# Linear attention in one kernel of two transformer blocks: both heads of a level written into two PSUM banks, their products alternating between the row halves of the tensor engine, with new scheduling priorities

## Chip, cores and metric

One Trainium2 chip, one of its cores. The metric is the device time of one execution in microseconds (us), as the median of several runs.

## What is computed

The program runs two blocks one after the other on 256 tokens of width 1024, in float32, with two layers in each block. The first block mixes three attentions per layer and is touched by the change only through the order of its instructions. In the second block a layer projects its input, hands the pieces to three mixers (GLA, a gated linear attention; RWKV7, a delta-rule recurrence; NSA, a sparse attention), joins their outputs in one output projection, and ends with a feed-forward network. GLA is what the change rewrites:

```python
def _gla_mixer(q, k, v, g, a_lr, w_a2, b_a, ln_w, ln_b):
    log_a = jax.nn.log_sigmoid((a_lr @ w_a2 + b_a).astype(f32)) / GLA_TAU
    ...
    def step(state, inp):
        qi, ki, vi, ai = inp
        b = jnp.cumsum(ai, axis=2)
        inter = jnp.einsum('bhtk,bhkv->bhtv', qi * jnp.exp(b), state)
        diff = b[:, :, :, None, :] - b[:, :, None, :, :]
        decay = jnp.exp(jnp.where(causal, diff, -jnp.inf))
        scores = jnp.einsum('bhtk,bhsk,bhtsk->bhts', qi, ki, decay)
        intra = jnp.einsum('bhts,bhsv->bhtv', scores, vi)
        ...
    o = _head_norm(o, ln_w, ln_b, H, LN_EPS)
    return (o * jax.nn.silu(g.astype(f32))).astype(dt)
...
        mix = jnp.concatenate([o_gla, o_rwkv, o_nsa], axis=-1) @ w_out[l]
```

## The kernel before

Nearly all of the time is matrix products on the tensor engine (PE). A float32 product with a weight is split into three products of a high and a low part (`mm3`, L353 to L357), and ScalarE (ACT) and VectorE (DVE) split each weight tile (`whi` at L321, `wlo` at L298) before it is used. L298 is a helper for all two-operand vector operations and L446 one for all transposes, so both lines collect many operations, and the names of the tiles tell them apart.

A framework orders the instructions. Each instruction gets a priority from its place in the program and from a table of offsets, `AHEAD`: a section opened with `self.sec("x")` is moved ahead by the number under "x", and it is moved back when that is negative. In a layer of the second block (`block2_layer`) four generators, for RWKV7, GLA, NSA's direct part and NSA's compressed part, are stepped by `side_by_side`: the one with the smallest clock goes next, and a generator's `yield d` moves its own clock by d. What the scheduler makes of it is a fixed order of instructions on each engine. Whatever stands behind a waiting instruction on its engine waits too.

GLA handles its 256 tokens without a chunk loop. `gla` (L1217) goes through eight levels, m = 1, 2, 4, ..., 128; in level m a block of 2m tokens attends from its upper half to its lower half. A level makes the tile `g_E`: two subtractions on DVE, an exponential on ACT (L1245), two multiplications on DVE, by `g_q` and `g_k`. The four heads of 64 channels lie in two tiles of 128 partitions (index c) by two halves of 64 partitions (index j). A product contracts over 64 partitions, so it uses half the rows of PE: rows 0 to 63 for j = 0, rows 64 to 127 for j = 1. For each j, four products (two token tiles tt by two c; L1258, and L1256 in the level m = 64; two in the level m = 128) go into one PSUM bank, and the new entries are then merged into `g_S[j]`, which holds the scores: by a masked copy on DVE (L1266) in the first five levels, by copies on ACT in the last three (L1263, L1260, L1270). When all levels are done, twelve products (L1277, L1278) make GLA's output o, `head_norm` (L877 to L893, with one operation on POOL at L890) and a multiplication by `g_g` make `yg`, and `out_feat` (L1169) transposes `yg` and splits it for the output projection. RWKV7 does the same with `yr`, and NSA with `yn`.

PSUM has eight banks. In the second block two of them form a pair for the pool `pp`, two a pair for `pr`, three are single banks (`pa`) and one is `pg`, which `psg` hands out. `psp` hands out one bank of the pair `pp`, `two` both of them. The projections, the RWKV7 levels and the output projection use the pair too: the output projection accumulates its four output pieces in two banks of `pa` and in the two banks of the pair `pp`, and its inputs come in the order NSA's two halves, `yr`, `yg`. In the kernel before, GLA has the bank `pg` for its levels, for o and for the transposes of `yg`.

```python
            for j in range(2):
                pr = slice(64 * j, 64 * j + 64)
                ps = self.psg(2, 2, 128)
...
                yield 2
        o = self.psg(2, 256)
```

Of the kernel before, what the change touches and what calls it, by code (L numbers as in the profile page):

```python
# [151 lines left out]
class Kern:  # L152
# [1047 lines left out]
    def gla_decay(self, alr, P):  # L1200

        nc = self.nc
        z = self.low_rank(self.psg, P, P_TAIL, 64, 80, alr)
        zb = self.c3("g_z")
        for c in range(2):
            nc.vector.tensor_scalar(zb[:, c], z[:, c], P[:, P_BA + c:P_BA + c + 1], None, op0=ALU.add)
        az = self.c3("g_az")
        nc.scalar.activation(az, zb, AF.Abs)
        nc.scalar.activation(az, az, AF.Exp, scale=-1.0)
        nc.scalar.activation(az, az, AF.Ln, bias=1.0)  # L1210
        self.stt(zb, zb, 0.0, az, ALU.min, ALU.subtract)
        b = self.c3("g_b")
        for c in range(2):
            nc.vector.tensor_tensor_scan(b[:, c], self.one.to_broadcast([128, 256]), zb[:, c], 0.0, ALU.mult, ALU.add)
        return b

    def gla(self, ins, b, rows, out):  # L1217

        nc = self.nc
        mm = nc.tensor.matmul  # L1220
        cst = self.c
        q, k, v, g2 = ins
        ST = [self.u("g_S", 2, 2, 128) for j in range(2)]
        qk = self.c3("g_E")
        nc.gpsimd.tensor_tensor(out=qk, in0=q, in1=k, op=ALU.mult)
        ps = self.psg(2, 2, 2)
        for tt in range(2):
# [9 lines left out]
        for lv in range(8):  # L1237
            m = 1 << lv
# [8 lines left out]
            self.tt_(view(E, 0), view(E, 0), view(k, 0), ALU.mult)  # L1247
            for j in range(2):
                pr = slice(64 * j, 64 * j + 64)
                ps = self.psg(2, 2, 128)  # L1250
                self.busy(f"gla{j}", ps[:, 0], ps[:, 1])
                for tt in range(2 if m < 128 else 1):
                    for c in range(2):
                        a, e = (E[pr, c, 128 * t:128 * t + 128] for t in ((tt, tt) if m < 128 else (0, 1)))
                        if m == 64:
                            mm(ps[0:64, tt, c, 0:64], a[:, 0:64], e[:, 64:128], start=tt + c == 0, stop=tt + c == 2)  # L1256
                        else:
                            mm(ps[:, tt, c], a, e, start=tt + c == 0, stop=c == 1 and (tt == 1 or m == 128))  # L1258
                if m == 64:
# [9 lines left out]
                else:  # L1269
                    nc.scalar.copy(off[:, j], ps[:, 0])  # L1270
                yield 2
        o = self.psg(2, 256)
        for h in range(4):
            j, c = h % 2, h // 2
# [211 lines left out]
    def block2_layer(self, l, xT):  # L1486
        nc = self.nc
        P = self.act.tile([128, P_N], F32, name="P2")
# [37 lines left out]
        def gla():  # L1526
            yield from self.gla_inputs(l, xT.w, made["g"])
            b = self.gla_decay(tl, P)
            yield 6
            for t in self.gla(made["g"], b, rows, yg):  # L1530
                yield t
            with self.sec("ofg"):
                feats["g"] = self.out_feat([yg[:, 0], yg[:, 1]], 0.5, self.psg)

# [191 lines left out]
}.items() for n in names.split()}  # L1726
AHEAD = dict(x=-107, x2=-267, m01=254, n12=1422, h1=368, n3=-94, rwkv=0, cmp=0, w=-330, h2=785, ww=-366, out=-225, gla=0, ofg=442, ln2=18, atta=-78, tok=336, imask=-209, rx1=-82, attb=590, rxf=526, w1=15, feat=5, nsa=0, ofn=326, rx0=25, hw=499, ofr=-116, hd=675, rin=10, wo=-72, ln1=298, t_side=-3, t_group=8, t_gin=20, t_gla=0, t_dir=-5, t_cmp=-10, side=-42)
KEEP = dict(lev=2, nsa=1, gla0=0, gla1=0, wo=3, rms00=0, rms01=0, rms10=0, rms11=0, ln100=0, ln101=0, ln110=0, ln111=0, ln200=0, ln201=0, ln210=0, ln211=0, start=0)
# [72 lines left out]
```

## Time and profile before

| | before |
|---|---|
| three runs, us | 1562.68, 1556.77, 1562.52; median 1562.52 |
| the profiled execution, us | 1556.73; its span 1554.9; mean granted clock of PE 0.988 |
| PE busy | 1492.6 us, 96% of the span |
| weight loads of PE (PEld) | 1286.2 us, 83% |
| DVE busy | 938.9 us, 60% |
| ACT busy | 710.6 us, 46% |
| POOL busy | 50.0 us, 3% |
| DMA | 231.69 MB, 149 GB/s on average |

How to read it: busy times are sums over one execution, on engines that run at the same time, so they don't add up to the span. PE's busy time is near the span, but its ends are modelled and products are pipelined, so what a product costs is read from the distance between the starts of neighbours, not from its own duration. A float32 product appears as two records. The three runs lie at two levels, one near the profiled execution and one 5.8 us above it.

### The profile page before, as it was taken

The page shows a single profiled execution, that of the slowest core. Times are in us where ns is not written, and L with a number is a line of the kernel's source. Part 1 is how long each engine was busy: PE and PEld are TensorE (multiplying, and loading weights), DVE is VectorE, ACT ScalarE, POOL GpSimd, SP SyncE. Part 2 cuts the span into 40 slices and gives each one's busy share as a digit, 9 for nine tenths or more (in the row PEclk, how much of TensorE's full clock was granted, in tenths as well). Part 3 has the DMA queues.
Part 4 walks back from the last instruction along what each step waited for, and adds up shares of the span by engine and source line. Part 5 has one row for each costly group of instructions (what it writes and reads, how often), then busy time and mean ns, then how long its engine had stood idle before and what let it go on. Part 6 is the DMA issues. An engine that isn't in the chain of part 4 may idle for free.

```text
span 1554.9 us, 26032 instructions
## 1 busy us (share of the span) xinstructions
PE 1492.6 (96%) x10502; PEld 1286.2 (83%) x10502; DVE 938.9 (60%) x1531; ACT 710.6 (46%) x1286; POOL 50.0 (3%) x82
## 2 busy tenths in 40 slices
PE   6999999999999999999999989999999999899997
PEld 5877899988787999868767769998888677789986
DVE  5586565565686655565367475556754675755564
ACT  5545554445454444444454334444454544344451
POOL 0000000000000000000011010000000010100000
PEclk9999999999999999999999999999999999999999
DMA  7743435445444445556710245556447101445560
GB/s 254 235 147 122 150 122 189 158 156 180 166 149 131 149 136 182 167 152 201 249 34 2 80 142 176 188 172 224 139 146 254 42 1 42 144 164 191 181 215 27
DMA packets 72984, 231.69 MB, mean 149 GB/s; under 512 B 8736, under 2 KB 11552, under 8 KB 72864
## 3 DMA queue, kind: packets, MB, share of 16 engines
q1 hardware_dynamic: 67248, 219.74, 42.8%
q10 hardware_dynamic: 5616, 10.30, 2.1%
q8 instruction: 82, 1.34, 0.3%
q14 instruction: 38, 0.31, 0.1%
HBM read 228.96 MB, written 1.05 MB: 148 GB/s over the span
## 4 chain that ended last, share of the span: by engine, by line
PE 46%; DVE 4%; DMA 3%; ACT 2%; issue 1%; POOL 0%; DVEq 0%; ACTq 0%; SPq 0%
PE ps L357 10%; PE ps L355 10%; PE ps L356 10%; PE ps L353 4%; DMA raw<-in_stream_dram 2%; PE ps L446 2%; PE ps L1258 2%; PE ps L613 1%; PE ps L656 1%; DVE wlo L298 1%; ACT whi L321 1%; PE ps L438 1%; PE ps L867 1%; PE ps L1052 0%; PE ps L1001 0%
## 5 line engine op out<-in xcount | busy, mean ns | idle before, releaser
L298 DVE TENSOR_TENSOR wlo<-raw,whi 128x1024 fp32r<-128x1024 f32 (+2 forms) x364 | 428.1, 1183 | 313.3 <-ACT whi L321 306.2
L321 ACT CAST whi<-raw 128x1024 fp32r<-128x1024 f32 (+2 forms) x364 | 367.8, 1018 | 403.9 <-PE ps L356 206.4
L355 PE MATMUL ps<-xTh,whi 128*128 128x256 f32 x720 | 205.5, 285 | 4.4 <-ACT whi L321 4.4
L357 PE MATMUL ps<-xTh,wlo 128*128 128x256 f32 x720 | 205.5, 285 | 1.5 <-DVE wlo L298 1.5
L356 PE MATMUL ps<-xTl,whi 128*128 128x256 f32 x720 | 205.1, 285 | 0.0
L357 PE MATMUL ps<-hTh,wlo 128*128 128x256 f32 x640 | 182.4, 285 | 0.0
L355 PE MATMUL ps<-hTh,whi 128*128 128x256 f32 x640 | 181.7, 284 | 0.0
L356 PE MATMUL ps<-hTl,whi 128*128 128x256 f32 x640 | 181.5, 284 | 0.0
L355 PEld LDWEIGHTS ps<-xTh,whi 128*128 128x128 f32 x720 | 138.8, 193 | 6.1 <-ACT whi L321 4.8
L357 PEld LDWEIGHTS ps<-xTh,wlo 128*128 128x128 f32 x720 | 138.8, 193 | 2.0 <-DVE wlo L298 1.9
L356 PEld LDWEIGHTS ps<-xTl,whi 128*128 128x128 f32 x720 | 138.7, 193 | 0.8
L356 PEld LDWEIGHTS ps<-hTl,whi 128*128 128x128 f32 x640 | 122.6, 191 | 1.1 <-issue 0.7
L355 PEld LDWEIGHTS ps<-hTh,whi 128*128 128x128 f32 x640 | 122.6, 192 | 0.7
L357 PEld LDWEIGHTS ps<-hTh,wlo 128*128 128x128 f32 x640 | 122.6, 192 | 0.4 <-issue 0.3
L355 PE MATMUL ps<-whi,hTh 128*128 128x512 f32 (+2 forms) x256 | 97.3, 380 | 1.1 <-ACT wi L772 1.1
L357 PE MATMUL ps<-whi,hTl 128*128 128x512 f32 (+2 forms) x256 | 97.0, 379 | 0.0
L356 PE MATMUL ps<-wlo,hTh 128*128 128x512 f32 (+2 forms) x256 | 95.9, 375 | 0.8 <-DVE wlo L298 0.8
L355 PE MATMUL ps<-whi,xTh 128*128 128x512 f32 (+1 forms) x144 | 55.1, 383 | 4.0 <-ACT xTh L425 2.5
L355 PEld LDWEIGHTS ps<-whi,hTh 128*128 128x128 f32 x256 | 48.1, 188 | 11.8 <-issue 3.3
L355 PE MATMUL ps<-whi,f_h 128*128 128x512 f32 x144 | 57.1, 396 | 0.0
L356 PE MATMUL ps<-wlo,f_h 128*128 128x512 f32 x144 | 57.0, 396 | 0.0
L357 PE MATMUL ps<-whi,f_l 128*128 128x512 f32 x144 | 56.9, 395 | 0.0
(474 smaller groups left out, 2898.1 us busy)
## 6 DMA issues: line engine op xcount, KB each, us to landing
raw<-in_stream_dram SPq DMA_DIRECT2D x346, 512.0 KB, 4.2
raw<-in_stream_dram SPq DMA_DIRECT2D x56, 256.0 KB, 3.1
whi<-in_stream_dram SPq DMA_DIRECT2D x11, 512.0 KB, 5.9
wlo<-in_stream_dram SPq DMA_DIRECT2D x11, 512.0 KB, 6.5
row<-in_ln_w_dram ACTq DMA_DIRECT2D x8, 256.0 KB, 4.0
row<-in_ln_b_dram ACTq DMA_DIRECT2D x8, 256.0 KB, 4.6
raw<-in_stream_dram SPq DMA_DIRECT2D x4, 480.0 KB, 3.8
raw<-in_stream_dram SPq DMA_DIRECT2D x4, 420.0 KB, 5.4
```

The source lines that it names most:

```text
L298: self.nc.vector.tensor_tensor(out=out, in0=a, in1=b, op=op)
L321: nc.scalar.copy(hi[:, :b - a], raw)
L353: mm(out, a, b, start=start, stop=stop)
L355: mm(out, a[0], b[0], start=start, stop=False)
L356: mm(out, a[0], b[1], start=False, stop=False)
L357: mm(out, a[1], b[0], start=False, stop=stop)
L438: self.nc.tensor.matmul(o, self.negb, self.causb[:, None, :].to_broadcast([128, n, 128]), start=True, stop=True)
L446: self.nc.tensor.transpose(pt[:, j], s, self.ident)
L613: nc.tensor.matmul(o[:, ocol(h)], ps[:, i * nk + k, :], vt(k, h), start=first and i == 0 and k == 0, stop=last and i == nh - 1 and k == nk ...
L656: nc.tensor.matmul(s3[:, i], qT[pr, h // 2], kT(pr, h, 128 * nk), start=i == 0, stop=False)
L867: self.nc.tensor.matmul(ps[:, c], P[r0:r1, off + 128 * c:off + 128 * c + 128], rhs[r0:r1], start=c == 0, stop=c == 1)
L1258: mm(ps[:, tt, c], a, e, start=tt + c == 0, stop=c == 1 and (tt == 1 or m == 128))
```

## The change

1. The low-rank decay of GLA, the diagonal of the scores, o and the transposes of `yg` move from the bank `pg` to a bank of the pair `pp`.
2. In a level both heads j get a bank each, the two banks of the pair `pp`, and j becomes the innermost loop: the eight products of a level (four in the last) alternate between the rows 0 to 63 and the rows 64 to 127 of PE. The merging operations of both heads follow, and one `yield 4` takes the place of two `yield 2`. The removed `busy` calls issued nothing (their counts in `KEEP` are 0).
3. Eight numbers of `AHEAD` change, so that the order changes in the first block, at the start and in GLA.

```diff
-        z = self.low_rank(self.psg, P, P_TAIL, 64, 80, alr)
+        z = self.low_rank(self.psp, P, P_TAIL, 64, 80, alr)
...
-        ps = self.psg(2, 2, 2)
+        ps = self.psp(2, 2, 2)
...
-            for j in range(2):
-                pr = slice(64 * j, 64 * j + 64)
-                ps = self.psg(2, 2, 128)
-                self.busy(f"gla{j}", ps[:, 0], ps[:, 1])
-                for tt in range(2 if m < 128 else 1):
-                    for c in range(2):
+            two = [p.rearrange("p (a b k) -> p a b k", a=2, b=2) for p in self.two(self.pp)]
+            for tt in range(2 if m < 128 else 1):
+                for c in range(2):
+                    for j in range(2):
+                        pr = slice(64 * j, 64 * j + 64)
                         a, e = (E[pr, c, 128 * t:128 * t + 128] for t in ((tt, tt) if m < 128 else (0, 1)))
                         if m == 64:
-                            mm(ps[0:64, tt, c, 0:64], a[:, 0:64], e[:, 64:128], start=tt + c == 0, stop=tt + c == 2)
+                            mm(two[j][0:64, tt, c, 0:64], a[:, 0:64], e[:, 64:128], start=tt + c == 0, stop=tt + c == 2)
                         else:
-                            mm(ps[:, tt, c], a, e, start=tt + c == 0, stop=c == 1 and (tt == 1 or m == 128))
+                            mm(two[j][:, tt, c], a, e, start=tt + c == 0, stop=c == 1 and (tt == 1 or m == 128))
+            for j, ps in enumerate(two):
...
-                yield 2
-        o = self.psg(2, 256)
+            yield 4
+        o = self.psp(2, 256)
...
-                feats["g"] = self.out_feat([yg[:, 0], yg[:, 1]], 0.5, self.psg)
+                feats["g"] = self.out_feat([yg[:, 0], yg[:, 1]], 0.5, self.psp)
```

Of `AHEAD` these change: x2 -267 to 185, gla 0 to -9, atta -78 to -518, tok 336 to 241, feat 5 to 7, rx0 25 to 45, ofr -116 to -604, t_gin 20 to 28. In the changed kernel the products of the levels are at L1257 (m = 64: L1255); nearly all other lines keep their numbers.

What moves, at three places of the first layer of the second block. An order says what stands behind what on an engine, and in brackets which engines' semaphores an instruction waits for.

First place: PE, in the GLA levels. Before, from one head of a level over other work to the next head (L656 and L659 are NSA's scores, L446 `r_P` transposes of RWKV7, L1064 its products):

```order
L1258 MATMUL ps<-g_E 128x128 [waits DVE_49]
L1258 MATMUL ps<-g_E 128x128 x3
L656 MATMUL ps<-n_kw,n_qT 128x256 x2
L659 LDWEIGHTS negb
L659 MATMUL ps<-causb,negb 128x2x128
L446 MATMUL ps<-c_ident,r_P 128x128 [waits DVE_49]
L446 MATMUL ps<-c_ident,r_P 128x128 x3
L1258 MATMUL ps<-g_E 128x128 [waits DVE_49]
L1258 MATMUL ps<-g_E 128x128 x3
L1064 MATMUL ps<-r_P,r_M 64x64 [waits Activation_49]
```

Now, the second and the third level (L1102 and L1106 are products of RWKV7's solution, `pexp` belongs to NSA):

```order
L1257 MATMUL ps<-g_E 128x128 [waits DVE_49,PE_49,Activation_49]
L1257 MATMUL ps<-g_E 128x128 x7
L1102 MATMUL ps<-r_rhs,r_Q 64x64 [waits PE_49,Activation_49]
L1102 MATMUL ps<-r_rhs,r_Q 64x64 x7
L446 MATMUL ps<-c_ident,pexp 128x128 x2
L656 MATMUL ps<-n_kw,n_qT 128x256 x2
L1257 MATMUL ps<-g_E 128x128 [waits DVE_49,PE_49]
L1257 MATMUL ps<-g_E 128x128
L1106 MATMUL ps<-r_WU,r_M 64x64 [waits DVE_49]
L1106 MATMUL ps<-r_WU,r_M 64x64 x3
L1257 MATMUL ps<-g_E 128x128 x3
```

The four products of a head have become the eight of a level. The levels now begin after the last RWKV7 level (the last L1064); before, the first five of them lay between its levels. Two levels, the third and the sixth, are broken into pieces by other work.

Second place: DVE, the masked copies. Before, from the first head of the second level to the second head of the third:

```order
L1266 COPY_PREDICATED g_S<-c_mgla,ps 128x512 [waits PE_49,Pool_49]
L298 TENSOR_TENSOR g_E<-g_b 128x32x8 x2
L298 TENSOR_TENSOR r_P<-ps,r_P 128x2x4x64 [waits PE_49]
L298 TENSOR_TENSOR g_E<-g_E,g_q 128x32x8 [waits Activation_49]
L1266 COPY_PREDICATED g_S<-c_mgla,ps 128x512 [waits PE_49]
L298 TENSOR_TENSOR g_E<-g_E,g_k 128x32x8 [waits DVE_49]
L595 TENSOR_REDUCE mx<-ps 128x2 [waits PE_49]
L597 TENSOR_SCALAR nb<-mx 128x2 [waits DVE_49]
L1266 COPY_PREDICATED g_S<-c_mgla,ps 128x512 [waits PE_49]
```

Now, the first and the second level:

```order
L1266 COPY_PREDICATED g_S<-c_mgla,ps 128x512 [waits PE_49,Pool_49]
L1266 COPY_PREDICATED g_S<-c_mgla,ps 128x512 [waits Pool_49]
L298 TENSOR_TENSOR g_E<-g_E,g_q 128x64x4 [waits Activation_49]
L298 TENSOR_TENSOR g_E<-g_E,g_k 128x64x4 [waits DVE_49]
L298 TENSOR_TENSOR g_E<-g_b 128x32x8 x2
L298 TENSOR_TENSOR g_E<-g_E,g_q 128x32x8 [waits Activation_49]
L298 TENSOR_TENSOR g_E<-g_E,g_k 128x32x8 [waits DVE_49]
L1266 COPY_PREDICATED g_S<-c_mgla,ps 128x512 [waits PE_49]
L1266 COPY_PREDICATED g_S<-c_mgla,ps 128x512
```

The two copies of a level now stand together, in all five levels that have them.

Third place: PE, in the output projection, where its inputs from RWKV7 and GLA come in. Before, `yg` was transposed some 40 rows earlier, and 34 products of 128x512 stand between the last product of RWKV7 (L1162) and this:

```order
L355 MATMUL ps<-whi,xTh 128x512
L356 MATMUL ps<-wlo,xTh 128x512
L357 MATMUL ps<-whi,xTl 128x512
L446 MATMUL ps<-c_ident,yr 128x128 [waits DVE_49,PE_49]
L446 MATMUL ps<-c_ident,yr 128x128
L355 MATMUL ps<-xhi,oh 128x512 [waits Activation_49]
L356 MATMUL ps<-xlo,oh 128x512
L355 MATMUL ps<-xhi,oh 128x512
L446 MATMUL ps<-c_ident,yr 128x128 [waits DVE_49]
L446 MATMUL ps<-c_ident,yr 128x128
```

Now 21 such products, the level m = 128 and o stand between L1162 and the first transposes of `yr`, then these and 12 products that use them, and then (`whi,xTh` are the first products into the pair `pp`):

```order
L446 MATMUL ps<-c_ident,yr 128x128 x2
L446 MATMUL ps<-c_ident,yg 128x128 [waits DVE_49]
L446 MATMUL ps<-c_ident,yg 128x128
L446 MATMUL ps<-c_ident,yg 128x128 [waits DVE_49]
L446 MATMUL ps<-c_ident,yg 128x128
L355 MATMUL ps<-whi,xTh 128x512 [waits DVE_49]
L356 MATMUL ps<-wlo,xTh 128x512
L357 MATMUL ps<-whi,xTl 128x512
```

The transposes of `yg` have moved behind `yr`, and half of the projection of NSA's output, 24 products, behind them, since the pair is in use by GLA until then. In the first block, attention A (section atta) moves about 250 rows back on PE, in front of which other projections are drawn; at the start two constants are loaded some ten places earlier on SP's queue.

## Rows read from the trace of the kernel before

**Rows 1.** The page, part 1: busy time of each engine.

```profile
PE 1492.6 (96%) x10502; PEld 1286.2 (83%) x10502; DVE 938.9 (60%) x1531; ACT 710.6 (46%) x1286; POOL 50.0 (3%) x82
```

**Rows 2.** Windows, layer 1: window, length, PE, PEld, DVE, ACT, POOL busy; clock; DMA.

```profile
840.00:860.00 20.00, 19.77 (x274) 15.92 (x272) 15.24 (x34) 7.69 (x20) 0.00 (x0) 1.00 0.01 3
...
880.00:900.00 20.00, 19.27 (x91) 14.88 (x90) 13.54 (x25) 5.63 (x10) 3.84 (x7) 0.83 0.52 172
```

**Rows 3.** Groups by line, PE: the products of the levels; count of records.

```profile
L1258 PE MATMUL ps<-g_E 64*128 64x128 f32 x208 | 31.4, 287 | 0.8 <-DVE g_S L1266 0.5 <-ACT g_S L1260 0.4
...
L1256 PE MATMUL ps<-g_E 64*64 64x64 f32 x32 | 2.6, 221 | 0.0
```

**Rows 4.** Timeline of PE, layer 1: start, length of the run of records, operation.

```profile
850.22 1.16 PE L1258 MATMUL ps<-g_E 64*128 64x128 f32 x8
851.30 0.69 PE L1064 MATMUL ps<-r_P,r_M 64*64 64x64 f32 x32
```

**Rows 5.** Timeline of PE, first block: eight products that alternate between row halves.

```profile
113.26 1.16 PE L630 MATMUL ps<-kT,qT 64*128 64x128 f32 x16
114.35 0.60 PE L633 MATMUL ps<-causb,negb 128*128 128x512 bf16 x2
```

**Rows 6.** Groups by line, DVE: the masked copies.

```profile
L1266 DVE COPY_PREDICATED g_S<-c_mgla,ps 128x512 f32<-128x512 uint8 x20 | 14.6, 732 | 5.2 <-PE ps L1258 5.0
```

**Rows 7.** Timeline of DVE, layer 1, around one masked copy.

```profile
853.64 0.72 DVE L1266 COPY_PREDICATED g_S<-c_mgla,ps 128x512 f32<-128x512 uint8 x1
854.25 0.41 DVE L298 TENSOR_TENSOR g_E<-g_b 128x256 f32<-128x256 f32 x1
855.41 0.42 DVE L298 TENSOR_TENSOR g_E<-g_E,g_q 128x256 f32<-128x256 f32 x1 [0.76 <-ACT g_E L1245]
```

**Rows 8.** Waits of PE in layer 1, 790 to 925: us, times, longest.

```profile
PE ps L446 <- DVE yr L298: 2.5, 1, 2.5
...
PE ps L446 <- DVE r_P L298: 1.0, 1, 1.0
...
PE ps L1159 <- ACT r_g L1144: 0.7, 1, 0.7
...
PE ps L613 <- ACT ptsb L610: 0.7, 1, 0.7
PE ps L355 <- ACT oh L428: 0.5, 1, 0.5
```

**Rows 9.** Waits of PE in layer 2, 1215 to 1345.

```profile
PE ps L446 <- DVE yr L298: 1.8, 1, 1.8
```

**Rows 10.** Timeline of PE, layer 1: o, then RWKV7's last products and `yr`.

```profile
872.36 0.56 PE L1277 MATMUL ps<-g_v,g_S 128*128 128x64 f32 x4
...
874.98 0.39 PE L446 MATMUL ps<-c_ident,pexp 128*128 128x128 f32 x2
...
892.95 0.66 PE L1162 MATMUL ps<-r_Z,r_RW 128*128 128x128 f32 x4
...
900.75 0.39 PE L356 MATMUL ps<-wlo,xTh 128*128 128x512 f32 x1
900.98 0.39 PE L357 MATMUL ps<-whi,xTl 128*128 128x512 f32 x1
903.84 0.41 PE L446 MATMUL ps<-c_ident,yr 128*128 128x128 f32 x2 [2.48 <-DVE yr L298]
...
907.36 0.63 PE L357 MATMUL ps<-xhi,ol 128*128 128x512 f32 x1
907.78 0.63 PE L355 MATMUL ps<-whi,oh 128*128 128x512 f32 x1
```

**Rows 11.** Timeline of DVE, layer 1: `yg` and the last operation on `yr`.

```profile
884.44 0.68 DVE L298 TENSOR_TENSOR yg<-g_yn,g_g 128x512 f32<-128x512 f32 x1
...
903.00 0.69 DVE L298 TENSOR_TENSOR yr<-r_yn,r_g 128x512 f32<-128x512 f32 x1
```

**Rows 12.** Timeline of POOL, layer 1: the operation inside the head norm of `yr`.

```profile
898.94 2.57 POOL L890 TENSOR_TENSOR hn<-hn,mhalf 128x8 f32<-128x8 f32 x1 [4.95 <-DVE hn L889]
```

More of the change, by code (lines that the diff above doesn't have):

```diff
@@ L1726 @@
 }.items() for n in names.split()}
-AHEAD = dict(x=-107, x2=-267, m01=254, n12=1422, h1=368, n3=-94, rwkv=0, cmp=0, w=-330, h2=785, ww=-366, out=-225, gla=0, ofg=442, ln2=18, atta=-78, tok=336, imask=-209, rx1=-82, attb=590, rxf=526, w1=15, feat=5, nsa=0, ofn=326, rx0=25, hw=499, ofr=-116, hd=675, rin=10, wo=-72, ln1=298, t_side=-3, t_group=8, t_gin=20, t_gla=0, t_dir=-5, t_cmp=-10, side=-42)
+AHEAD = dict(x=-107, x2=185, m01=254, n12=1422, h1=368, n3=-94, rwkv=0, cmp=0, w=-330, h2=785, ww=-366, out=-225, gla=-9, ofg=442, ln2=18, atta=-518, tok=241, imask=-209, rx1=-82, attb=590, rxf=526, w1=15, feat=7, nsa=0, ofn=326, rx0=45, hw=499, ofr=-604, hd=675, rin=10, wo=-72, ln1=298, t_side=-3, t_group=8, t_gin=28, t_gla=0, t_dir=-5, t_cmp=-10, side=-42)
 KEEP = dict(lev=2, nsa=1, gla0=0, gla1=0, wo=3, rms00=0, rms01=0, rms10=0, rms11=0, ln100=0, ln101=0, ln110=0, ln111=0, ln200=0, ln201=0, ln210=0, ln211=0, start=0)
```

## The prediction

> **What bounds the kernel now.** I read the page's busy times first. PE is busy for 1492.6 us, 96% of the span [rows 1], so time is saved by making PE's work shorter, and lost where PE waits. DVE stands at 60% over the whole, but the change sits in one stage, so I read that stage's windows next: where GLA's levels run, DVE is busy for 15.24 of 20 us beside 19.77 of PE [rows 2]. It is near the bound there. The groups by line give the size of the work that is changed: the products of the levels are 208 + 32 records, 31.4 + 2.6 us [rows 3], two records a product. Those durations overlap, so a product's price comes from starts in the timeline: eight records of one head begin at 850.22 and the next work at 851.30 [rows 4], 1.08 us for four products. The waits of PE say where it stands still today: at RWKV7's result `yr` 2.5 us in layer 1 and 1.8 in layer 2, and 0.5 to 1.0 us at four other places [rows 8, 9]; at the products of the levels 0.8 us over both layers [rows 3].
>
> **Products of the levels.** Two heads take 2 x 1.08 = 2.16 us a level today. The same shape alternating between the row halves is in the trace: 16 records, eight products, from 113.26 to 114.35 [rows 5], 1.09 us. So a level saves 1.07 us. Six levels are of this form: 6.4 us a layer. The level m = 128 has four products of the form, 4 x 0.27 = 1.08 us, and saves half, 0.55. The level m = 64 is 2.6 us over both layers [rows 3], and half of 1.3 a layer is 0.65; its starts are less regular, so I take 0.55. Together -7.5 us a layer. Two levels are broken by other work, and where a piece ends with one half alone the other half is unused; each such end costs at most half of the 0.27 of a product, I take 0.3 for both. [...]
>
> **Copies between the levels.** Before, head 0's copy ran while head 1's products ran, so PE had the cover in its own work. Now both copies follow the eight products, and the next level needs both banks back. A copy lasts 0.73 us [rows 6], and the next DVE operation starts 0.61 us after it (853.64 to 854.25 [rows 7]). So the banks come back 0.1 + 2 x 0.62 = 1.35 us after the products: a wait that replaces the one-bank wait, and behind it on PE stand RWKV7's and NSA's products as well. There are seven gaps. In full they are 7 x 1.35 = 9.5 us a layer; with cover everywhere they are nothing. The order shows what stands in them: 0.2 to 1.5 us of RWKV7 and NSA work each, by the durations that these have today. Gap by gap I count 2.75 us uncovered, against 0.4 now. That is +2.4, nearer the lower end because only two gaps have almost no work in them. Both ends (0 and +9.1) stay for the range.
>
> **RWKV7's levels.** Five of them ran with GLA products between a DVE step and the product that needs it. That filler is gone, as the first GLA level now follows the last L1064. Such a step shows today as a wait of 1.0 us at `r_P` [rows 8]. NSA's work still fills; I take +0.5 a layer, between 0 and five such waits at half their length, 2.5.
>
> **The tail.** After RWKV7's last product (L1162, ending at 893.6) `yr` is ready at 903.7 [rows 10, 11], 10.1 us later, since its norm goes through six DVE steps, ACT and 2.57 us on POOL [rows 12]. Today 34 products at 0.23 (900.75 to 900.98 [rows 10]) cover 7.8 of it and PE waits 2.5 [rows 8]. Now 21 products (4.8), the last level (0.55, after 0.3 of waiting) and o (872.36 to 874.98 [rows 10], 2.6) cover 7.95, with 0.3 waited: about 1.85 is left. Then come the 0.5 for `oh` [rows 8] and twelve products, 2.8. Next late is `yg`. Its chain took from 874.98 to 885.1 [rows 10, 11], 10.1 us too. It now starts 4.35 us behind the chain of `yr` and shares DVE and POOL with it, so I put it at 15.4 after L1162, where PE is ready at 13.9: +1.5. Its own split delays the first product into the pair by about 1.0 (0.5 for `oh`, 0.4 for the DVE half). The sum is 0.3 + 1.85 + 0.5 + 1.5 + 1.0 = 5.15 us. The waits that it replaces are, in layer 1, 2.5 + 0.7 + 0.7 + 0.5 = 4.4 [rows 8], the two of 0.7 covered by the late levels; in layer 2, where the wait for `oh` doesn't show, 1.8 + 0.7 + 0.7 = 3.2 [rows 8, 9]. That is +0.75 and +1.95, on average +1.4.
>
> **The rest.** The first block's moved rows and the loads at the start replace covered work by covered work: projection products stand in front of the delayed attention as they did before it. I set this to 0, and bound it by a wait as long as the longest in these rows, 2.5, either way. `gla`, `t_gin`, `feat` and `rx0` act through the order already counted.
>
> **Sum.** Per layer -7.5 + 0.3 + 2.4 + 0.5 + 1.4 = -2.9; two layers -5.8. Against the profiled execution's 1556.73 that is 1550.9. The runs lie at 1556.8 and at 1562.6, and the changed kernel may show either level, so I take half of the 5.8 between them: **1553.8 us**, 0.56% under the median of 1562.52, which is 5.8 above the profiled time. A difference of 0.5%, 7.8 us, is about what a measurement of this kernel can tell from none.
>
> **Rivals.**
>
> A, the full gain. If all copies are covered and the tail costs no more than now, -7.5 + 0.3 = -7.2 a layer, 1542.3 by the profiled time, 1545 measured. For it: work of two other mixers stands in most gaps. Against it: DVE at 15.24 of 20 [rows 2].
>
> B, DVE bounds the levels. A level costs DVE four operations of about 0.34 and two copies of 0.62, 2.6 us, more than twice its products' 1.09. Packed behind RWKV7 the levels would then wait for DVE twice as long as I count: 4.8 in place of 2.4, -0.5 a layer, 1555.7, measured 1558.6. For it: the copies stand together, and a `g_E` wait of 0.76 on DVE itself [rows 7]. Against it: DVE has 4.8 idle us in those 20. [...]
>
> C, slower: the two norm chains come one after the other. `yg`'s operations queue on DVE and POOL behind those of `yr`, so `yg` comes 8.6 us after `yr` (its 10.1 less the first reduction and its neighbours, 1.5) and not 5.3, and PE, with 3.5 us of work there, stands still for 3.3 more. PE's granted clock then falls to half, where a product's starts are 0.42 apart (907.36 to 907.78 [rows 10]), as it was in that layer after the wait for `yr`. Half of the 48 products behind at 0.20 more are 4.8. A layer is then -2.9 + 3.3 + 4.8 = +5.2: 1567.1, measured 1570. It decides where `yg` is over 2.9 us later than I put it, less with a fallen clock. For it: 24 products left the place in front of `yr`. Against it: the order puts most of `yg`'s steps in the pauses of `yr`'s chain.
>
> [...]
>
> E, the clock falls within the levels. If the many short waits at the pair bring a stretch at half clock like that of 880 to 900, where the clock was 0.83 and 3.4 us were lost [rows 2], a layer is +0.5: 1557.7, measured 1560.6. Against it: 1.00 at 840 to 860, with short waits too. [...]
>
> **How the numbers follow.** Forecast 0.38, A 0.20, B 0.16, C 0.13, D 0.05, E 0.08. The forecast's own range is 1548 to 1559 (the rest's 2.5 and half the distance of the levels). Its threshold of 1554.7 lies close, so it gives 0.22 to faster and 0.16 to the same. A gives faster 0.19, same 0.01; B 0.02, 0.13 and slower 0.01; C same 0.03, slower 0.10; D same 0.04, slower 0.01; E faster 0.01, same 0.06, slower 0.01. Together 0.44, 0.43, 0.13. The range of 8 in 10 is 1543 to 1565: it takes in A down to its profiled time and the bounds of the copies in part, and leaves out C.
>
> **What would show it.** Eight products of a level in 1.1 us of start to start, and about 17 us less busy time at the products' lines; waits of PE at the products for `g_S` of 2 to 4 us a layer; a wait for `yr` below 2.5 and a new one for `yg` of 1 to 2; granted clock 1.00 in the levels. I am wrong if the waits for `g_S` exceed 5 us a layer, if `yg` is waited for over 4 us, or if the first block ends over 2.5 us earlier or later.

## The result, and the profile after

The changed kernel takes **1576.46 us** (median of 4 runs, 1569.86 to 1583.47) against 1559.9 for the kernel before beside it (4 runs): a ratio of 1.0134, with 95% interval [1.0101, 1.0168]. It is slower, by 1.3%. The forecast was 1553.8, its range 1543 to 1565.

The page, part 1 and a line of part 2, of the profiled execution of the changed kernel (1578.37 us, span 1576.6):

```profile
PE 1503.8 (95%) x10502; PEld 1290.4 (82%) x10502; DVE 939.0 (60%) x1531; ACT 712.3 (45%) x1286; POOL 47.3 (3%) x82
...
PEclk9999999999999999999998889999999988899999
```

Beside [rows 1], PE is busy for 11.2 us more, although the products were to become cheaper. They did; groups by line, PE and DVE:

```profile
L1257 PE MATMUL ps<-g_E 64*128 64x128 f32 x208 | 23.5, 349 | 2.9 <-DVE g_S L1266 2.5 <-DVE r_WU L1112 0.4
...
L1255 PE MATMUL ps<-g_E 64*64 64x64 f32 x32 | 1.4, 224 | 0.0
...
L1266 DVE COPY_PREDICATED g_S<-c_mgla,ps 128x512 f32<-128x512 uint8 x20 | 13.4, 720 | 7.5 <-PE ps L1257 7.4
```

31.4 and 2.6 us [rows 3] have become 23.5 and 1.4. But one record now lasts 349 ns, not 287, and the waits for `g_S` are 2.5 us over both layers. The 349 goes with the two dips in the PEclk row, in the slices of the span where GLA's levels and the output projection of each layer lie. The windows (start and end, length, busy time of PE, PEld, DVE, ACT and POOL with counts, granted clock, DMA share, GB/s) show it, first of the kernel before (the first block; layer 1's levels and output projection; layer 2's):

```profile
0.00:640.00 640.00, 621.65 (x4323) 550.92 (x4324) 398.28 (x661) 317.15 (x557) 9.86 (x17) 1.00 0.50 164
800.00:930.00 130.00, 120.75 (x1107) 95.79 (x1107) 92.25 (x189) 51.27 (x114) 13.28 (x19) 0.96 0.22 69
1220.00:1370.00 150.00, 141.06 (x1185) 109.21 (x1185) 101.41 (x200) 59.19 (x131) 11.08 (x9) 0.95 0.19 61
```

The same windows of the changed kernel, and four shorter ones, around its falls of the clock in layer 1:

```profile
0.00:640.00 640.00, 618.42 (x4277) 548.76 (x4278) 395.10 (x659) 315.84 (x555) 9.92 (x17) 1.00 0.50 163
800.00:930.00 130.00, 118.34 (x1070) 88.61 (x1069) 82.34 (x169) 47.58 (x105) 11.89 (x18) 0.91 0.15 49
1220.00:1370.00 150.00, 138.27 (x1164) 101.98 (x1162) 95.16 (x197) 62.16 (x145) 11.35 (x14) 0.91 0.11 37
...
851.00:859.00 8.00, 8.00 (x88) 5.11 (x91) 5.29 (x12) 2.21 (x7) 1.31 (x2) 0.57 0.01 3
864.00:880.00 16.00, 15.54 (x107) 12.93 (x108) 9.16 (x23) 4.33 (x11) 0.00 (x0) 0.68 0.01 1
909.00:917.00 8.00, 6.67 (x18) 5.03 (x19) 1.42 (x3) 2.00 (x3) 0.00 (x0) 0.57 0.06 18
929.00:938.00 9.00, 7.59 (x24) 5.96 (x25) 7.79 (x14) 1.18 (x2) 0.56 (x1) 0.62 0.39 130
```

The first block is at 1.00 in both, so the loss lies in the mixers' stages: 0.91 there, where it was 0.96 and 0.95. In the short windows the granted clock lies between the two levels that its records in these traces show, 1.00 (as from 860 to 864 in the changed kernel) and 0.50 (852 to 858), since each begins or ends with some time at the upper one. The changed kernel falls to the lower level four times in each layer's mixers and output projection; the kernel before did so twice in each. Summed over windows of 1 us, it stands at the lower level for 80.6 us, the kernel before for 38.6.

That gives a split of the time. Span times mean clock is about what the execution would last at the upper level: an estimate, since it lets all work stretch with the clock. Before, it is 1554.9 x 0.988 = 1536.2 us; after, 1576.6 x 0.975 = 1537.2. So **nearly all of the 21.7 us between the two spans is clock** (39.4 us lost to it against 18.7), and the product saving is also gone. Both need a cause. The other executions agree: span times clock is 1534 to 1537 us in the four of the changed kernel, and 1532 to 1538 in 82 of the kernel before, which ran beside the experiments and took 1548.5 to 1574.5 us at granted clocks of 0.993 to 0.976.

What PE did ahead of the falls is in its timeline (start, length, operation, idle before it and what ended that); the changed kernel, layer 1:

```profile
847.18 0.95 PE L1229 MATMUL ps<-c_ones,g_E 128*128 128x2 f32 x8
849.99 1.10 PE L613 MATMUL ps<-n_vw,ptsb 128*128 128x64 f32 x8 [1.86 <-ACT ptsb L610]
...
856.94 1.71 PE L1257 MATMUL ps<-g_E 64*128 64x128 f32 x16
...
860.26 1.16 PE L1257 MATMUL ps<-g_E 64*128 64x128 f32 x16 [0.38 <-DVE g_S L1266]
861.35 0.68 PE L1102 MATMUL ps<-r_rhs,r_Q 64*64 64x64 f32 x16
...
864.33 0.49 PE L1257 MATMUL ps<-g_E 64*128 64x128 f32 x4 [0.87 <-DVE g_S L1266]
...
908.03 0.44 PE L446 MATMUL ps<-c_ident,yg 128*128 128x128 f32 x2 [1.24 <-DVE yg L298]
909.40 0.69 PE L446 MATMUL ps<-c_ident,yg 128*128 128x128 f32 x2 [0.93 <-DVE ol L301]
911.02 0.79 PE L355 MATMUL ps<-whi,xTh 128*128 128x512 f32 x1 [0.93 <-DVE ol L301]
```

At the clock's upper level the eight products of one of GLA's levels take 1.09 us from their start to the next work, as forecast (860.26 to 861.35); inside the first fall the run of the same products lasts 1.71 us, in place of 1.16 (856.94). A new wait of 1.86 us at `ptsb` ends 1.3 us before the first fall, which the clock's records put at 851.3. The second, at 864.9, comes right behind 0.38 and 0.87 us at `g_S`. 3.1 us of waits in three pieces at `yg` and its split stand around the start of the third, and the fourth, at 929.8, follows a wait of 2.2 us at `dn`, the sum that is normalized after the output projection. The waits of PE from 840 to 935 (total, times, longest), to be set beside [rows 8]:

```profile
PE ps L446 <- DVE dn L301: 2.2, 1, 2.2
PE ps L613 <- ACT ptsb L610: 1.9, 1, 1.9
PE ps L1257 <- DVE g_S L1266: 1.3, 2, 0.9
PE ps L446 <- DVE yg L298: 1.2, 1, 1.2
PE ps L446 <- DVE ol L301: 0.9, 1, 0.9
PE ps L355 <- DVE ol L301: 0.9, 1, 0.9
PE ps L1141 <- DVE r_Z L298: 0.9, 1, 0.9
...
PE ps L446 <- DVE yr L298: 0.4, 1, 0.4
```

Layer 2 shows the same waits within 0.1 us, but none at `yr`. The one at `ptsb` has its cause on ACT, here in the changed kernel:

```profile
845.01 1.28 ACT L1210 ACT_TABLE_LOAD   x1
846.31 0.63 ACT L1210 ACTIVATE g_az<-g_az 128x512 f32<-128x512 f32 x1
847.15 1.28 ACT L601 ACT_TABLE_LOAD   x1 [0.21 <-DVE nb L597]
```

One table load stands ahead of the decay's logarithm, another ahead of NSA's exponential: 2 x 1.28 us. The new numbers put this pair of loads in front of an NSA block that PE then needs at once.

### The profile page after: what moved, and what is told of

Same layout as the page of the kernel before. It is cut to its first block, busy times and chain, and to the rows that moved or that the text cites. A ratio compares the mean times of both kernels' runs of the same rounds, so it can differ in the third digit from the quotient of the medians.

```text
span 1576.6 us, 26065 instructions
## 1 busy us (share of the span) xinstructions
PE 1503.8 (95%) x10502; PEld 1290.4 (82%) x10502; DVE 939.0 (60%) x1531; ACT 712.3 (45%) x1286; POOL 47.3 (3%) x82
## 4 chain that ended last, share of the span: by engine, by line
PE 79%; DVE 8%; ACT 6%; DMA 4%; issue 2%; POOL 0%; SPq 0%; ACTq 0%; DVEq 0%; POOLq 0%
PE ps L355 19%; PE ps L356 19%; PE ps L357 19%; PE ps L446 4%; PE ps L353 3%; DMA raw<-in_stream_dram 3%; PE ps L613 2%; ACT pexp L571 2%; PE ps L656 2%; ACT whi L321 2%; DVE wlo L298 1%; PE ps L583 1%; PE ps L641 1%; PE ps L1257 1%; DVE mx L563 1%
## 5 line engine op out<-in xcount | busy, mean ns | idle before, releaser
L355 PE MATMUL ps<-whi,xTh 128*128 128x512 f32 (+1 forms) x144 | 58.6, 407 | 5.7 <-ACT xTh L425 2.5
L357 PE MATMUL ps<-whi,xTl 128*128 128x512 f32 (+1 forms) x144 | 57.0, 396 | 0.1
```

The costliest lines, as they stand in the source:

```text
L355: mm(out, a[0], b[0], start=start, stop=False)
L357: mm(out, a[1], b[0], start=False, stop=stop)
```

## The experiments

Three questions: whether the edit of the products or the new numbers cost the time; which of the numbers; and what alternation is worth. Gains and costs are differences of the ratios, each against the kernel before on the same chip, times 1555 us. Of the numbers (`AHEAD`) the diffs show the changed entries alone. Windows and waits are those of one profiled execution of each kernel.

**The new code with the old numbers**

```diff
-x2=185, gla=-9, atta=-518, tok=241, feat=7, rx0=45, ofr=-604, t_gin=28
+x2=-267, gla=0, atta=-78, tok=336, feat=5, rx0=25, ofr=-116, t_gin=20
```

> The new GLA code with the old priorities: the eight levels stand among RWKV7's levels again, unbroken, and yg is transposed before yr. Theory P (the place: the new priorities put GLA's decay and its levels behind RWKV7, PE then waits 1.9 us for ptsb, 1.3 for g_S and about 4 at the output projection, and the clock falls around these waits): no wait for ptsb above 0.8 us, at most 45 us at half clock in all (before 38.6, the change 80.6), time 1541 to 1552. Theory S (sharing the pair, with both copies behind the products, makes the falls whatever the priorities): over 60 us at half clock, g_S waits of 2 us a layer or more, time 1565 to 1580.

1569.8 us, ratio 1.0088 [1.007, 1.0106]. The products' starts sum to 16.8 us over both layers, where they were 30.7: the saving of 13.9 is there. It goes at two waits of PE, window 780 to 930 of this kernel:

```profile
PE ps L446 <- DVE yr L298: 7.2, 1, 7.2
PE ps L446 <- DVE yg L298: 3.1, 1, 3.1
```

So the edit in the code alone is slower too, with waits that the new numbers shorten (0.4 and 1.2 with them). The waits take back the saving, and the rest is clock: over the ten executions the median of span times clock is 1536.5 us, that of the kernel before beside them 1536.6, but 31.4 us are lost to the clock against 17.1. I had expected either a faster kernel or waits for `g_S` of 2 us a layer; the time is in the second range, but `g_S` is waited for 0.8 us in layer 1, so neither account held.

**The new numbers with the old code**

```diff
-x2=-267, gla=0, atta=-78, tok=336, feat=5, rx0=25, ofr=-116, t_gin=20
+x2=185, gla=-9, atta=-518, tok=241, feat=7, rx0=45, ofr=-604, t_gin=28
```

> The old GLA code (one bank, heads in turn, products not alternating) with the new priorities. Theory P: the wait for ptsb of about 1.9 us a layer and at least three clock falls a layer appear here too, time 1575 to 1592 (the products' 15 us are not saved). Theory S: no more than 45 us at half clock, time 1555 to 1565.

1630.6 us, 1.0457 [1.0369, 1.0544], far above both expectations. Two windows of it:

```profile
855.00:921.00 66.00, 66.00 (x367) 51.32 (x366) 27.13 (x59) 15.49 (x36) 0.88 (x1) 0.51 0.08 27
...
1316.00:1365.00 49.00, 49.00 (x311) 39.06 (x310) 21.36 (x47) 10.24 (x24) 1.27 (x2) 0.51 0.00 1
```

The profile shows PE busy without a gap for 66 and for 49 us, at the lower clock nearly all the time. Each half of the change alone is slower than the kernel before, and both times the loss is mostly clock.

**The heads in turn, in the same two banks**

```diff
-            for tt in range(2 if m < 128 else 1):
-                for c in range(2):
-                    for j in range(2):
+            for j in range(2):
+                for tt in range(2 if m < 128 else 1):
+                    for c in range(2):
```

> The changed kernel with the two loops exchanged: head 0's products first, then head 1's, in the same two banks; every instruction keeps its place on its engine but the eight products of a level are not alternating. If the alternation saves what its starts show (1.08 us a level) and nothing is given back: 10 to 16 us slower than the change, about 1588 to 1592. Theory Q (the shorter products only lengthen the waits behind them and bring the clock falls): within 5 us of the change, 1572 to 1581, with fewer falls.

1588.16 us, 1.018 [1.0105, 1.0255]. Its windows, against those of the changed kernel above:

```profile
851.00:859.00 8.00, 8.00 (x60) 5.19 (x60) 5.15 (x11) 2.03 (x7) 1.41 (x2) 0.52 0.01 3
859.00:864.00 5.00, 5.00 (x83) 4.66 (x81) 2.88 (x7) 1.95 (x6) 0.00 (x0) 0.50 0.00 0
864.00:880.00 16.00, 16.00 (x96) 12.87 (x94) 6.79 (x16) 3.61 (x9) 0.00 (x0) 0.54 0.00 1
```

The fall begins at the same `ptsb` wait, and where the alternating kernel is back at the upper level by 859, this one stays low until 879. The runs of the two kernels don't overlap (1586.69 to 1594.7 against 1569.86 to 1583.47), but the intervals of their ratios do. So alternation looks worth having in this place, but an order so sensitive to the clock can't tell the products' own price.

**o and the transposes of `yg` back in the one bank `pg`**

```diff
-        o = self.psp(2, 256)
+        o = self.psg(2, 256)
...
-                feats["g"] = self.out_feat([yg[:, 0], yg[:, 1]], 0.5, self.psp)
+                feats["g"] = self.out_feat([yg[:, 0], yg[:, 1]], 0.5, self.psg)
```

> The changed kernel with o and the transposes of yg back in the bank pg, so that the output projection's second pair is free earlier. Theory P: the falls at 909 to 917 and 1349 to 1357 go or shrink, the waits at yg and ol (3.1 us a layer) shrink to under 1.5, the falls in the levels stay: 6 to 12 us faster than the change, 1564 to 1571. Theory S' (all the loss is in the levels): within 4 us of the change.

1567.51 us, 1.0083 [1.0061, 1.0106]: 8 us better than the changed kernel. The fall at 909 to 917 is shorter (913 to 917); in layer 1 both falls in the levels stay, with the `ptsb` wait still 1.9, and in layer 2 one of the two. The waits at `yg` and its split, which I had expected to shrink, sum to 2.2 + 1.2 = 3.4 us, against 3.1: the 8 us are clock, not shorter waits. So the tail is one part, and the greater part lies in the levels.

**The first block's old numbers in the changed kernel**

```diff
-x2=185, atta=-518, tok=241, feat=7, rx0=45
+x2=-267, atta=-78, tok=336, feat=5, rx0=25
```

> The changed kernel with the old priorities of the first block and the start (x2, rx0, atta, tok, feat) and the new ones of the mixers (gla, t_gin, ofr). Theory P (the place of GLA's levels and the tail cause the loss): the four falls of the clock a layer stay, time within 6 us of the change, 1570 to 1582. If the first block's order matters: 1560 to 1568.

1569.7 us, 1.0098 [1.0069, 1.0126]: about 5.6 less than the change, between its two expectations. Of the eight falls of both layers' mixers seven are there in its profile, and two new ones.

**The levels alone: old numbers, tail in `pg`**

```diff
-        o = self.psp(2, 256)
+        o = self.psg(2, 256)
...
-                feats["g"] = self.out_feat([yg[:, 0], yg[:, 1]], 0.5, self.psp)
+                feats["g"] = self.out_feat([yg[:, 0], yg[:, 1]], 0.5, self.psg)
...
-x2=185, gla=-9, atta=-518, tok=241, feat=7, rx0=45, ofr=-604, t_gin=28
+x2=-267, gla=0, atta=-78, tok=336, feat=5, rx0=25, ofr=-116, t_gin=20
```

> Old priorities, alternating levels in the pair, but o and the transposes of yg in the bank pg as before. The run with the old table and all of the new code waited 7.2 us at yr in each layer and 4.2 at yg, and its products of the levels took 13.9 us less. Theory T (there the loss is the pair, held for yg's transposes, which took the output projection's filler from in front of yr): the wait for yr falls back to 2 to 3 us, half clock to under 45 us, time 12 to 20 us below the kernel before, 1535 to 1545. Theory S (the levels in the pair cost what they save, through the two copies and the projections that use the pair): within 5 us of the kernel before.

**1543.32 us, 0.9925 [0.9897, 0.9952]**: faster than both kernels. (The low-rank decay and the diagonal of the scores are in the pair here too, as in the change.) The windows and groups:

```profile
800.00:930.00 130.00, 118.09 (x1138) 93.64 (x1138) 96.52 (x194) 54.30 (x120) 13.97 (x19) 0.99 0.23 73
1220.00:1370.00 150.00, 138.02 (x1258) 110.92 (x1258) 106.86 (x208) 61.56 (x132) 11.01 (x9) 0.98 0.23 78
```

```profile
L1257 PE MATMUL ps<-g_E 64*128 64x128 f32 x208 | 17.3, 285 | 1.6 <-DVE g_S L1266 1.5
```

The clock is 0.99 and 0.98, above the kernel before, the products take 17.3 us, and `g_S` is waited for 0.8 us a layer. `yr` is waited for 2.5 us in layer 1, as before.

**The same with the first block's new numbers**

```diff
-x2=-267, atta=-78, tok=336, rx0=25
+x2=185, atta=-518, tok=241, rx0=45
```

> The kernel of the label e7 with the new priorities of the first block and the start (x2, rx0, atta, tok) and the old ones of the second block's mixers (gla, t_gin, ofr, feat). If the first block's order is worth nothing either way, within 3 us of e7. If the moved attention costs what the change's longer waits at L583 show (3.8 against 1.3 us), 2 to 6 us slower than e7.

1548.07 us, 0.996 [0.9937, 0.9982]: 5.4 worse than without, the same size as undoing them gave (5.6). It is not clock: the medians of what is lost to it are 15.5 and 15.4 us. In the first block the wait of PE for `pexp` grows from 1.3 to 3.8 us, and the block's last products (`mh`) start 3.8 us later (684.81 against 680.96); the rest of the 5.4 I did not find.

**The tail alone, in the kernel before**

```diff
-        o = self.psg(2, 256)
+        o = self.psp(2, 256)
...
-                feats["g"] = self.out_feat([yg[:, 0], yg[:, 1]], 0.5, self.psg)
+                feats["g"] = self.out_feat([yg[:, 0], yg[:, 1]], 0.5, self.psp)
```

> The kernel before with one part of the change: o and the transposes of yg in a bank of the pair instead of pg. Theory T: waits at yg and yr grow by 4 us or more a layer, 8 to 16 us slower than the kernel before. Theory S: within 4 us of it.

1554.5 us, 0.9997 [0.9969, 1.0025]: nothing. The tail in the pair costs only where the levels are in it as well.

**One number: `t_gin` in the kernel with the levels alone**

```diff
-t_gin=20
+t_gin=28
```

> The kernel of the label e7 with one number of the priorities changed, t_gin 20 to 28, which by itself puts GLA's decay and all levels behind RWKV7's last level. Theory P (the place of the levels is what costs): waits at ptsb of 1.9 us and at yg in each layer, 60 us or more at half clock, 15 to 25 us slower than e7, 1558 to 1568. Theory R (it takes the three numbers of the mixers together): within 8 us of e7.

1557.92 us, 0.9977 [0.995, 1.0004]: 8 us worse than 0.9925 (13 by the medians). Windows of this kernel, from an execution of 1561.36 us, the longest of its eleven:

```profile
800.00:930.00 130.00, 120.16 (x1053) 91.28 (x1054) 89.48 (x177) 49.09 (x108) 12.95 (x19) 0.91 0.22 69
1220.00:1370.00 150.00, 139.78 (x1179) 105.54 (x1179) 101.27 (x205) 57.56 (x132) 11.89 (x14) 0.91 0.17 57
```

and waits of PE, 780 to 930:

```profile
PE ps L446 <- DVE dn L301: 2.1, 1, 2.1
PE ps L613 <- ACT ptsb L610: 1.9, 1, 1.9
...
PE ps L1257 <- DVE g_S L1266: 1.2, 2, 0.9
PE ps L446 <- DVE yg L298: 1.2, 1, 1.2
```

This one entry brings the changed kernel's waits at `ptsb`, `g_S` and `yg` and, in this execution, its 0.91. PE's idle time over the whole span is not more (64.2 us against 65.6 without it), and span times clock is not longer either (1559.6 x 0.977 = 1523.7 against 1537.7 x 0.992 = 1525.4). The idle time only lies in other places, and the clock falls. Over all executions the medians say the same: 1526.9 against 1525.4 of span times clock, and 29.6 us lost to the clock against 15.4. The entry moves GLA's decay, its table loads and all levels together; which of them matters it does not tell.

**The heads in turn, where the clock is good**

```diff
-            for tt in range(2 if m < 128 else 1):
-                for c in range(2):
-                    for j in range(2):
+            for j in range(2):
+                for tt in range(2 if m < 128 else 1):
+                    for c in range(2):
```

> The kernel of the label e7 (levels in the pair, old priorities, tail in pg) with the heads' products one after the other instead of alternating; every instruction keeps its place on its engine. Theory P (where PE does not wait behind the levels, the alternation is worth its starts, 1.08 us a level and 13.9 us over both layers): 12 to 18 us slower than e7, 1555 to 1562, about the kernel before. Theory Q (part of the gain is only more waiting): 4 to 9 us slower than e7.

1548.71 us, 0.9952 [0.9916, 0.9989], against 0.9925 alternating. The intervals overlap. The timeline is clear; of this kernel:

```profile
840.04 1.71 PE L1257 MATMUL ps<-g_E 64*128 64x128 f32 x16
841.68 0.57 PE L1072 MATMUL ps<-r_X,r_Q 64*64 64x64 f32 x22
```

and of the alternating one:

```profile
837.41 1.16 PE L1257 MATMUL ps<-g_E 64*128 64x128 f32 x16
838.50 0.57 PE L1072 MATMUL ps<-r_X,r_Q 64*64 64x64 f32 x22
```

From start to start a level takes 1.64 us with its heads in turn and 1.09 alternating; it was 2 x 1.08 = 2.16 [rows 4] with other work between the heads. So of the gain in the products' starts half (7.0 of the 13.9 us, summed over all products) comes from two banks and adjacency alone, half from the alternation. In the kernel's time the alternation is worth less than its 6.9 us: 4 us by the ratios, and 2.8 by the medians of span times clock (1528.2 against 1525.4). I had expected 12 to 18 if the starts were all, and 4 to 9 if part of the gain only becomes waiting; the second is nearer.

**The logarithm replaced, to leave out its table loads**

```diff
-        nc.scalar.activation(az, az, AF.Ln, bias=1.0)
+        nc.scalar.activation(az, az, AF.Square, bias=1.0)
```

> The changed kernel without the logarithm of GLA's decay (a square stands in its place), so that ACT does not load its function table for it and back for NSA's exponentials, 2 x 1.28 us, which PE waited for at ptsb. Theory C (a wait of PE is what the falls of the clock follow): the wait at ptsb under 0.8 us, the falls at 851 and 1288 gone, 6 to 14 us faster than the change, 1562 to 1570. Theory C' (the levels' own products bring the falls): the falls stay within 5 us of where they are, at most 4 us faster.

1581.38 us, 1.0157 [1.0107, 1.0207]: no better. (With the square it computes something else; only its time is of use.) The `ptsb` wait is gone, but the timeline shows three others in its place:

```profile
851.67 0.66 PE L446 MATMUL ps<-c_ident,r_P 128*128 128x128 f32 x4 [1.15 <-DVE r_P L298]
...
853.48 0.69 PE L1064 MATMUL ps<-r_P,r_M 64*64 64x64 f32 x32 [1.16 <-ACT r_Q L1021]
...
855.56 2.04 PE L1257 MATMUL ps<-g_E 64*128 64x128 f32 x14 [1.06 <-DVE g_E L298]
```

The fall follows them, from 854.8 to 882.1. It does not tell whether the table loads as such matter: that stays open. Removing one wait let the next late result show.

**What of the tail costs: o, or the transposes?** Each put into the pair by itself, in the kernel with the levels alone:

```diff
-        o = self.psg(2, 256)
+        o = self.psp(2, 256)
```

> The kernel of the label e7 with GLA's output o in the pair, and yg's transposes left in pg. By its order o stands 30 rows later on PE, behind RWKV7's use of the pair, and only 5 products stand between L1162 and yr in place of 34. Theory O (o is the part of the tail that costs: it queues for the pair, yg comes late, and PE stands at yg in front of RWKV7's last products): waits at yr of 7 us or more in each layer, at yg of 1 to 3, time 1562 to 1575. Theory Y (the transposes of yg are what costs): within 5 us of e7, 1539 to 1549.

```diff
-                feats["g"] = self.out_feat([yg[:, 0], yg[:, 1]], 0.5, self.psg)
+                feats["g"] = self.out_feat([yg[:, 0], yg[:, 1]], 0.5, self.psp)
```

> The kernel of the label e7 with yg's transposes in the pair, and o left in pg. Its order keeps o, yg and yr in the places of e7. Theory O: within 5 us of e7, 1539 to 1549. Theory Y: waits at yr of 7 us, time 1562 to 1575.

o in the pair: 1563.22 us, 1.0049 [1.0023, 1.0074], 19 us worse than 0.9925. The transposes: 1545.81 us, 0.9936 [0.9903, 0.9969], no difference that can be told. With o in the pair, a wait of PE from 780 to 930 reads:

```profile
PE ps L446 <- DVE yr L298: 8.3, 1, 8.3
```

With the levels in `pg` (the tail alone, above) PE waits for `yr` 2.5 us and at `yg` not at all. With levels and o both in the pair, o stands behind RWKV7's use of it, some 30 rows later on PE. `yg` comes late, PE stands at it, for 2.8 us with o in the pair, *in front of* RWKV7's last products (L1153, L1159, L1162), and these start the chain of `yr` late as well. The new numbers mend that by putting `yg` behind `yr`, and pay in the levels.

**The account, by ratios.** From the kernel before: the levels alone, 0.9925, -11.7 us. The first block's numbers, to 0.996, +5.4. The mixers' numbers (`gla`, `t_gin`, `ofr`, `feat`), to 1.0083, +19.1, of which `t_gin` by itself gave 8. The tail in the pair, to 1.0134, +7.9. Together +20.8.

What each step costs in work and waits, and what in clock, is told by the same split: the medians over all executions of span times clock, and of the rest of the span, each less that of the kernel before on the same chip (for the last row, less that of its profiled execution). These are estimates, good to about 1 us, as the clock is recorded with three digits.

| us against the kernel before | span times clock | lost to the clock |
|---|---|---|
| the levels alone | -8.8 | -3.2 |
| and the first block's numbers | -3.4 | -3.1 |
| and the mixers' numbers | -1.2 | +14.2 |
| and the tail in the pair: the change | -1.1 | +19.9 |

The first block's numbers cost 5.4 us of work and no clock; the mixers' numbers cost 17.3 us of clock and 2.2 of work, and the tail 5.7 of clock alone.

## Why the prediction was wrong

**The products** were right. Forecast 2 x (7.5 - 0.3) = 14.4 us; measured 13.9 at an undisturbed clock, and 7.3 in the changed kernel, where falls of the clock lie on the products. With the levels alone the kernel is at 1543.3, about the price of rival A (1545). D, that the alternation would save less than [rows 5] promise, fell: a level takes 1.09, as there.

**The copies** were right in kind and over-priced: `g_S` is waited for 1.3 us in layer 1 and 1.2 in layer 2, not 2.75. (The bound of seven gaps was too wide as well: the masked copies stand in five levels only.) So B fell: 0.8 to 1.3 us of such waits a layer stand beside 6.9 saved.

**RWKV7's levels** were forecast at +0.5 a layer. The wait of 1.0 us at `r_P` [rows 8] is 0.2 in layer 1 of the changed kernel; one of 0.9 at `r_Z` is new. The size was harmless.

**The tail** was near: `yr` 0.4 (I had 1.85), `oh` 0.5 (0.5), `yg` 1.2 (1.5), the splits 0.9 + 0.9 (1.0); 3.9 in place of 5.15. That the order of the new numbers repairs a place that the new code spoils could have been seen only with the old numbers beside it: 7.2 + 3.1 us in layer 1 there.

**The clock is the step that failed.** In "What would show it" I set the granted clock to 1.00 in the levels, and rival E's price to one fall of 3.4 us lost a layer, at a chance of 0.08. Four falls came in layer 1 alone, and the whole kernel lost 39.4 us to the clock where it had lost 18.7: about 10 us more a layer. By the order in time E was right for the second fall, which follows `g_S` and the pair; the first follows `ptsb`, which no rival had. C's second half (a fall in the output projection, after waits at `yg`) came too, with a wait of 1.2 rather than 1.5 + 3.3. Each was sized as if only one fall a layer could come, and C as if it needed a long wait ahead of it; I also argued from 1.00 at 840 to 860 [rows 2], which the kernel before kept with one wait of 0.23 us at `g_S` in that stretch. The changed order has 1.86 us at `ptsb` there.

**"`gla`, `t_gin`, `feat` and `rx0` act through the order already counted"** failed with it. I counted, in the order, only the gaps between GLA's own levels. `t_gin` also moves the two table loads of the decay on ACT in front of NSA's exponential. That wait, with the fall behind it, I had not priced at all. `t_gin` alone turned 0.99 and 0.98 into 0.91 in both layers of the profiled execution. That the table loads are what does it is not shown: with the logarithm replaced, and no wait at `ptsb` left, the changed kernel was no faster.

**The rest**, 0 with a bound of 2.5, failed too: the first block's numbers cost about 5.4, outside the bound, and this is not clock. The `pexp` wait is 2.5 of it; the other part is not settled. The sign that I had named came: the first block's last products (`mh`) start at 685.25 in the changed kernel, 681.61 before, 3.6 us later. The 2.9 us that I added for two levels of the runs had little ground: the 82 further executions of the kernel before do not keep to two levels, their times follow the granted clock.

Rival E put a fall in the levels down to the many short waits at the pair. The second fall does follow such waits, 0.38 and 0.87 us at `g_S`. But the kernel with the levels alone uses the same two banks, waits for `g_S` 0.8 us a layer and is at 0.99 and 0.98: the pair by itself did not bring the fall.

What stays open is which idle time a fall follows. Apart from the one at the end of the program, those of the changed kernel follow 1.2 to 3.3 us of idle time of PE within a few microseconds; yet the kernel before waits 1.8 us at `yr` in layer 2 [rows 9] with no fall behind it, and the kernel with the levels alone has one short fall (898.0 to 901.4) behind its 2.5 us at `yr`. No run separates the single waits.

## What to carry to other kernels

Split a difference first into clock and the rest, by span times mean granted clock of both kernels' executions; here that one product showed that 20.7 of the 21.7 us lay in the clock, where the busy times read as "more work". When an order is searched anew together with an edit, run each half alone, and each part of the edit under the old order: the good part of this change was worth 0.75% and was hidden under an o in a bank that had another user, and under new numbers, one of which moved GLA's decay and levels behind RWKV7's. Where PE is the bound and a stage shows falls of the clock already, price a new wait with a stretch at the lower level behind it, one for each place (here four in layer 1, of 6.8 to 10.2 us each), and look for the late results of *other* mixers that a moved step pushes back on ACT and DVE.

## What was not expected of the hardware

- Two heads' products one after the other, each in its own row half and bank, already overlap: 1.64 us for the eight, between 2.16 apart and 1.09 alternating. I had expected 2.16 without alternation. The single records of the weight loads show how. Within a row half the weight loads start about 0.11 us apart, in the kernel before, with the heads in turn and alternating alike. With the heads in turn the second head's first load starts 0.55 us after the first head's (840.589 and 840.035), while two of the first head's eight are still to come; alternating, the loads of the two halves start in pairs, 6 to 7 ns apart (113.257 and 113.264 in the products of [rows 5]; 35 to 36 ns in the changed kernel's level at 860.26).
- Busy time by itself did not bring the clock back: from 855 to 921 in the old code with the new numbers, the profile, whose ends of products are modelled, shows PE busy for all 66.00 us, at a mean clock of 0.51.
- The same order of work after the same wait stayed at the lower level until 879 with the heads in turn and until 859 with the products alternating. Alternation alone does not decide it: without the logarithm the products alternate too, and that kernel stayed low from 854.8 to 882.1. What does was not tried.
